# Experts on whole float32 weight slabs in column tiles, 36 slabs in a ring

## The chip, the cores and the metric

The kernel runs on one core of one Trainium2 chip. A core has TensorE (PE in the profile) for matrix products, VectorE (DVE), ScalarE (ACT), GpSimd (POOL), SyncE (SP), whose queue issues most transfers here, and 16 DMA engines. The metric is the device time of one execution in microseconds (us); lower is better.

## The reference

One layer of a decoder trunk on 512 tokens of 1024 channels, float32: a gated mixer, a cross attention, and a mixture of 32 experts of which each token takes 4. Only the last part is touched by the change:

```python
logits = xt @ w_router + b_router                  # (512, 32)
top_val, top_idx = lax.top_k(logits, 4)
gate = softmax(top_val)
def expert_block(xi, e):
    gu = xi @ w_gu[e] + b_gu[e]                    # 1024 -> 2048
    x_glu, x_lin = gu[..., ::2], gu[..., 1::2]
    x_glu = minimum(x_glu, 7.0)
    x_lin = clip(x_lin, -7.0, 7.0)
    h = x_glu * sigmoid(1.702 * x_glu) * (x_lin + 1.0)
    return h @ w_dn[e] + b_dn[e]                   # 1024 -> 1024
# y[token] += gate * expert_block(x[token], e); then h = layer_norm(2**0.25 * h + y)
```

An expert has 12.6 MB of weights (403 MB in all 32), in 24 slabs of 512 KB: 16 for gate and up, 8 for down. A slab is 128 input channels by 1024 outputs. With the reference's inputs its router gives the experts these numbers of tokens, in order: 49, 68, 94, 45, 50, 119, 41, 117, 131, 65, 9, 83, 52, 80, 73, 31, 73, 22, 27, 67, 85, 38, 45, 42, 144, 15, 147, 49, 58, 72, 21, 36. So 17 experts have up to 64, ten have 65 to 96, two have 97 to 128 and three have more.

## The kernel before, in words

`dense` (line 807) computes everything up to the router; `experts` (line 1205) then goes through the 32 experts in order, whatever their counts; `finish` (line 1468) does the last layer norm.

*Tokens in, rows out.* `route_expert` turns one-hot rows (made on GpSimd by `one_hots`, line 983) into the indices and gates of an expert's tokens. An indirect DMA on the GpSimd queue gathers them (line 1030), TensorE transposes them (`tokens`, line 1118), and at the end another indirect DMA adds the expert's rows into the `based` tensor in memory (line 1037). For up to 64 tokens both move half rows, so that 128 partitions are used.

*Two ways for the products* (`products`, line 1132). The counts are loaded into registers, and each engine branches on them. Up to 64 tokens: the float32 slab as it came is streamed against 64 columns of tokens, the two halves of the output in the two column halves of TensorE (line 1155). More than 64: each slab is first split into a float32r high part (ScalarE) and a float32r low part (VectorE) by `split` (line 126), and three float32r products take the place of the float32 one (`mm3`, lines 156 to 160). Above 128 tokens, the rest goes through four more float32r products a slab with tokens and their low parts packed side by side (lines 1163 to 1169).

*Order of the work.* Inside a hand-ordered section, per turn e: gate/up half 0 of expert e, routing of e + 2, the activation of half 0, gate/up half 1, transposes of the tokens of e + 1, the activation of half 1, the down product of e - 1, transposes of the hidden units of e, and the rows of e - 1 out. Between them stand calls of `ahead`, which issue the splits of coming slabs.

*Slabs.* Loads of 512 KB are issued in order on the SP queue (line 186) into a ring of 17 raw buffers; the split slabs have 8 pairs of buffers. The bias rows are loaded first of all (line 1210), in float32r.

Of the kernel before, what the change touches and what calls it, by code (L numbers as in the profile page):

```python
# [109 lines left out]
class Trunk:  # L110
# [42 lines left out]
    def ps(self, name, tag="c", dt=F32, shape=(512,)):  # L153
        return self.psum.tile([128] + list(shape), dt, name=name, tag=tag, bufs={"tp": 2, "f": 2, "c": 4, "ga": 2, "gb": 2, "y": 2}[tag])
# [652 lines left out]
    def dense(self):  # L807
        nc, tc, a = self.nc, self.tc, self.a
        with ExitStack() as es:
# [9 lines left out]
            self.xs = self.xg[:, 0:512]  # L819
# [34 lines left out]
            def finish():  # L854
                while done:
                    b, t = done.pop(0)
                    self.router_block(b, t)
                    if b == 3:
                        self.first = self.route_expert(0, self.route, self.one_hots(0, self.route))
                        self.router_end()  # L860
                    self.base_block(b, t)
# [10 lines left out]
            finish()  # L872


    def router_init(self):
# [23 lines left out]
        pid2 = p.tile([128, 1], F32, name="pid2")  # L899
        nc.gpsimd.iota(pid2, pattern=[[0, 1]], base=0, channel_multiplier=2, allow_small_or_imprecise_dtypes=True)  # L900

        self.offs = p.tile([128, 1], F32, name="offs")
        nc.gpsimd.memset(self.offs[0:64], 2.0 * NONE)
        nc.gpsimd.memset(self.offs[64:128], 2.0 * NONE + 1)
        for b in range(4):
            nc.gpsimd.tensor_copy(self.VT[:, b, :, 0], pid.to_broadcast([128, 32]))
            nc.gpsimd.memset(self.VT[:, b, :, 1], 128.0 * b - NONE)
            nc.gpsimd.tensor_copy(self.VT[:, b, :, 5], pid2.to_broadcast([128, 32]))
            nc.gpsimd.memset(self.VT[:, b, :, 6], 2 * (128.0 * b - NONE))

        self.esel = p.tile([128, 2, 32], F32R, name="esel")
# [4 lines left out]
        for j in range(2):  # L916
            nc.vector.tensor_scalar(self.esel[:, j], e, 0.0, None, op0=OP.is_equal)
        for r, j in ((slice(0, 64), 1), (slice(64, 128), 0)):
            nc.vector.memset(self.esel[r, j].bitcast(F32), 0.0)
# [69 lines left out]
    def route_expert(self, e, pool, oh, bank="tp"):  # L989
# [3 lines left out]
        for n, c in ((128, 0), (CAP - 128, 16)):  # L993
            for b in range(4):
                nc.tensor.matmul(o[:n, c:c + 8], oh[:, b, 128 * (c > 0):128 * (c > 0) + n], self.VT[:, b, e, :],
                                 start=b == 0, stop=b == 3)
        for b in range(4):
            for r in (slice(0, 64), slice(64, 128)):
                nc.tensor.matmul(o[r, 8:16], oh[:, b, 0:64], self.VT[:, b, e, :], start=b == 0, stop=b == 3)  # L999
        return self.slot(o[:, 0:8], pool, "m"), self.slot(o[:CAP - 128, 16:24], pool, "x"), self.slot(o[:, 8:16], pool, "s")  # L1000

    def slot(self, o, pool, t):
# [3 lines left out]
        if t == "s":  # L1006
            nc.vector.tensor_scalar(ix, o[:, 5:6], o[:, 6:7], self.offs, op0=OP.add, op1=OP.add)
        else:
            nc.vector.tensor_scalar(ix, o[:, 0:1], o[:, 1:2], float(NONE), op0=OP.add, op1=OP.add)  # L1009
# [4 lines left out]
    def cond(self, c, *engines):  # L1014
        return self.nc.values_load(c[0:1, 0:1], engines=engines, min_val=0, max_val=512,
                                   skip_runtime_bounds_check_because="a count of the 512 tokens")

    def gather_expert(self, count, route):

        with self.tc.If(self.cond(count, mybir.EngineType.Pool) < 65) as s:  # L1020
            self.gather(self.xs, route[2][0], True)
        with s.Else():
            self.gather(self.xg, route[0][0])

    def rows_of(self, t, halves):
        return (t.rearrange("t (h c) -> (t h) c", h=2), 1023) if halves else (t, 511)

    def gather(self, xg, ix, halves=False):
        src, last = self.rows_of(self.x2d, halves)
        return self.nc.gpsimd.indirect_dma_start(  # L1030
            out=xg, out_offset=None, in_=src, in_offset=bass.IndirectOffsetOnAxis(ap=ix[:, 0:1], axis=0),
            bounds_check=last, oob_is_err=False).ins

    def scatter(self, y, ix, halves=False):

        dst, last = self.rows_of(self.based, halves)
        self.nc.gpsimd.indirect_dma_start(  # L1037
            out=dst, out_offset=bass.IndirectOffsetOnAxis(ap=ix[:, 0:1], axis=0), in_=y, in_offset=None,
            bounds_check=last, oob_is_err=False, compute_op=OP.add)
# [27 lines left out]
    def x_tiles(self, xg, x=None, part=(0, 1)):  # L1067

        nc = self.nc
        x = x or self.mx.tile([128, 8, 2, 128], F32R, name="xe", tag="xe", bufs=self.XB)  # L1070
        for g in part:
            self.turn4(x[:, 4 * g:4 * g + 4], xg[:, ts(g, 512)], "xt")
        return x

    def turn4(self, out, src, name):

        pt = self.ps(name, "tp")
        for j in range(4):
            self.nc.tensor.transpose(pt[:, ts(j, 128)], src[:, ts(j, 128)], self.ident)
        self.split(out[:, :, 0], out[:, :, 1], pt.rearrange("p (k t) -> p k t", t=128))  # L1080

    def swiglu(self, pg, pl, g, l):
        nc = self.nc
        nc.vector.tensor_scalar(g, pg, 7.0, None, op0=OP.min)  # L1084
        a = nc.scalar.activation(g, g, AF.Gelu_apprx_sigmoid)  # L1085
        nc.vector.tensor_scalar(l, pl, 7.0, -7.0, op0=OP.min, op1=OP.max)
        v = nc.vector.scalar_tensor_tensor(l, l, 1.0, g, op0=OP.add, op1=OP.mult)
        return a.ins, v.ins

    def hidden_units(self, rv, p, more):  # L1090

        tc = self.tc
        g, l = [self.mx.tile([128, 512], F32, name=n, tag=n, bufs=self.SB[n]) for n in ("mg", "ml")]
        with tc.If(rv < 65) as s:
            self.swiglu(p[0][0:64], p[0][64:128], g[:64], l[:64])
        with s.Else():
            self.swiglu(*p, g, l)
            with tc.If(rv > 128):
                self.more_swiglu(*more, g)
        return l  # L1100

    def hidden(self, rv, units):

        nc = self.nc
        out = [self.mx.tile([128, 4, 2, 128], F32R, name="hx", tag="hx", bufs=self.HB) for _ in units]
        whole = [self.mx.tile([128, 4, 64], F32, name="hs", tag="hs", bufs=self.HB) for _ in units]
        with self.tc.If(rv < 65) as s:
            for t, u in zip(whole, units):
                pt = self.ps("hts", "tp")
                for j in range(4):  # L1110
                    nc.tensor.transpose(pt[:, ts(j, 64)], u[:64, ts(j, 128)], self.ident[:64, :64])
                nc.scalar.copy(t.rearrange("p k t -> p (k t)"), pt[:, :256])
        with s.Else():
            for t, u in zip(out, units):
                self.turn4(t, u, "ht")
        return out, whole

    def tokens(self, rv):

        nc = self.nc  # L1120
        out = self.mx.tile([128, 8, 2, 128], F32R, name="xe", tag="xe", bufs=self.XB)
        whole = self.mx.tile([128, 8, 64], F32, name="xw", tag="xw", bufs=self.XB)
        with self.tc.If(rv < 65) as s:
            pt = self.ps("xts", "tp")
            for j in range(4):
                nc.tensor.transpose(pt[:, ts(j, 128)], self.xs[:, ts(j, 128)], self.ident)  # L1126
            nc.scalar.copy(whole.rearrange("p (h g) t -> p h g t", h=2), pt.rearrange("p (g h t) -> p h g t", g=4, h=2))
        with s.Else():
            self.x_tiles(self.xg, out)
        return out, whole  # L1130

    def products(self, rv, p, lhs, small, more, pm, ws, bias=None, pack=None):

        nc, tc = self.nc, self.tc
        mm = nc.tensor.matmul
        if bias:
            sel, row, w = self.esel, bias[0], bias[1]

        def first():
            for k in range(8):
                for n in range(2):
                    if k == 0 and bias:
                        mm(p[n], sel[:, n, row:row + 1].to_broadcast([128, 128]), w, start=True, stop=False)
                    self.mm3(p[n], (lhs(k)[:, 0], lhs(k)[:, 1]), [w[:, ts(n, 512)] for w in ws(k)[:2]],
                             k == 0 and not bias, k == 7)

        with tc.If(rv < 65) as s:  # L1149
            for n in range(2 if bias else 0):  # L1150
# [376 lines left out]
```

## Time and profile before

| | us |
|---|---|
| median of 3 runs | 1934.29 |
| lowest and highest | 1933.17, 1937.43 |
| the profiled execution | 1926.95 |
| its span, first to last instruction | 1925.2 |

The rows further down come from that profiled execution. Times are from the start of its span. In a row of a timeline stand start, duration, engine, line, operation, what it writes and reads, how many were merged, and in brackets the idle time before it and what ended that. In a table by line stand total and mean duration after the bar. A float32 matmul shows as two records, a float32r or bf16 one as one. Busy time of TensorE includes time at the lower clock.

### The profile page before, as it was taken

To read this page: it belongs to the slowest core of one execution; us is meant where nothing else is said; L and a number is where in the kernel's file an instruction comes from. 1 tells how busy PE (TensorE), PEld (TensorE's weight loads), DVE (VectorE), ACT (ScalarE), POOL (GpSimd) and SP (SyncE) were. 2 spreads that over 40 slices of the span, in tenths; PEclk is the share of its full clock that TensorE was granted. 3 is DMA by queue.
4 is the path that set the end of the run, shared out by engine and by line. 5 is a ranking of instruction groups with operands and counts; after the bars stand their busy time and mean duration, and the time that the engine had idled before them with its cause. 6 is when DMAs were issued, how large, how long until landed. Compare 5 with 4: busy or idle time off the path is not lost. (4 is left out here: it accounts for less than half of the span.)

```text
span 1925.2 us, 27343 instructions
## 1 busy us (share of the span) xinstructions
PE 1701.1 (88%) x8236; PEld 1164.7 (60%) x8236; DVE 1056.0 (55%) x1747; ACT 813.0 (42%) x1252; POOL 352.6 (18%) x414
## 2 busy tenths in 40 slices
PE   8998999999996688889998888998898899897982
PEld 7666878778984365456675646664564365653540
DVE  7855776567564375337683746663573245442433
ACT  5567555344431254226463535452462134332321
POOL 1010003410011221112121212212122111111002
PEclk9999999999996799899999989999898999898986
DMA  4213235655232888989777899999899959589994
GB/s 165 99 57 113 97 107 169 194 184 184 89 113 80 333 343 322 371 307 397 278 277 279 301 370 337 360 375 397 346 375 355 401 211 369 188 333 351 351 346 174
DMA packets 148184, 505.16 MB, mean 262 GB/s; under 512 B 19856, under 2 KB 22448, under 8 KB 147888
## 3 DMA queue, kind: packets, MB, share of 16 engines
q1 hardware_dynamic: 131952, 460.38, 62.8%
q0 software_dynamic: 15936, 40.96, 7.3%
q8 instruction: 170, 2.79, 0.6%
q14 instruction: 126, 1.03, 0.1%
HBM read 481.86 MB, written 28.84 MB: 265 GB/s over the span
## 5 line engine op out<-in xcount | busy, mean ns | idle before, releaser
L128 DVE TENSOR_TENSOR wlo<-raw,whi 128x1024 fp32r<-128x1024 f32 (+2 forms) x441 | 510.6, 1199 | 209.5 <-ACT whi L128 137.2
L128 ACT CAST whi<-raw 128x1024 fp32r<-128x1024 f32 (+2 forms) x441 | 432.2, 1025 | 238.6 <-PE gu L160 41.9
L1155 PE MATMUL gu<-raw,xw 128*64 128x512 f32 x1088 | 249.5, 611 | 0.0
L158 PE MATMUL gu<-whi,xe 128*128 128x512 f32 x480 | 194.7, 406 | 8.2 <-ACT whi L128 8.2
L159 PE MATMUL gu<-wlo,xe 128*128 128x512 f32 x480 | 194.0, 404 | 5.6 <-DVE mg L1084 4.3
L160 PE MATMUL gu<-whi,xe 128*128 128x512 f32 x480 | 193.6, 403 | 2.5 <-issue 2.5
L1155 PEld LDWEIGHTS gu<-raw,xw 128*64 128x64 f32 x1088 | 89.9, 142 | 157.9 <-issue 143.8
L986 POOL TENSOR_SCALAR oh<-places,pm 128x192 bf16<-128x192 bf16 x128 | 141.4, 1113 | 225.9 <-PE sl L999 203.2
L1085 ACT ACTIVATE mg<-mg 128x512 f32<-128x512 f32 (+1 forms) x70 | 44.2, 631 | 267.0 <-DVE mg L1084 259.2
L158 PE MATMUL y<-whi,hx 128*128 128x512 f32 x240 | 101.7, 424 | 29.7 <-ACT whi L128 17.0
L1155 PE MATMUL y<-raw,hs 128*64 128x512 f32 x544 | 122.2, 602 | 1.1 <-issue 1.1
L158 PEld LDWEIGHTS gu<-whi,xe 128*128 128x128 f32 x480 | 94.3, 196 | 31.6 <-ACT whi L128 8.6
L160 PEld LDWEIGHTS gu<-whi,xe 128*128 128x128 f32 x480 | 93.7, 195 | 27.2 <-issue 5.5
L159 PEld LDWEIGHTS gu<-wlo,xe 128*128 128x128 f32 x480 | 93.9, 196 | 23.0 <-DVE wlo L128 1.0
L160 PE MATMUL y<-whi,hx 128*128 128x512 f32 x240 | 100.1, 417 | 3.8 <-issue 3.8
L159 PE MATMUL y<-wlo,hx 128*128 128x512 f32 x240 | 100.0, 417 | 2.2 <-DVE wlo L128 2.2
L1009 DVE TENSOR_SCALAR ixm<-sl 128x1 int32<-128x1 f32 x32 | 7.0, 220 | 165.9 <-PE sl L999 161.3
L1084 DVE TENSOR_SCALAR mg<-gu 64x512 f32<-64x512 f32 (+1 forms) x64 | 43.4, 677 | 97.8 <-PE xts L1126 47.2
L1155 PEld LDWEIGHTS y<-raw,hs 128*64 128x64 f32 x544 | 38.9, 138 | 72.8 <-issue 62.8
L1037 POOL DMA_INDIRECT based<-ysb,ixm x15 | 24.2, 1611 | 283.1 <-ACTq L1345 137.1
L158 PEld LDWEIGHTS y<-whi,hx 128*128 128x128 f32 x240 | 48.7, 203 | 42.8 <-ACT whi L128 21.5
L1037 POOL DMA_INDIRECT based<-ysb,ixs x17 | 27.4, 1614 | 178.6 <-ACTq L1149 89.0
(500 smaller groups left out, 3191.9 us busy)
## 6 DMA issues: line engine op xcount, KB each, us to landing
raw<-in_wgu SPq DMA_DIRECT2D x512, 512.0 KB
raw<-in_wdn SPq DMA_DIRECT2D x256, 512.0 KB
raw<-in_wt SPq DMA_DIRECT2D x27, 512.0 KB
tgd<-tg POOLq DMA_DIRECT2D x16, 256.0 KB, 2.6
raw<-in_wck SPq DMA_DIRECT2D x8, 512.0 KB
tgr<-tgd POOLq DMA_DIRECT2D x16, 256.0 KB, 3.1
raw<-in_wmix SPq DMA_DIRECT2D x8, 512.0 KB
raw<-in_wcv SPq DMA_DIRECT2D x8, 512.0 KB
```

What stands on the lines that cost most here:

```text
L128: return nc.scalar.copy(hi, src).ins, (lo_eng or nc.vector).tensor_sub(lo, src, hi.bitcast(F32)).ins
L158: mm(out, w[0], x[0], start=start, stop=False)
L159: mm(out, w[0], x[1], start=False, stop=False)
L160: mm(out, w[1], x[0], start=False, stop=stop)
L986: self.nc.gpsimd.tensor_scalar(oh[:, b], self.places, self.pm[:, b, e:e + 1], None, op0=OP.is_equal)
L1009: nc.vector.tensor_scalar(ix, o[:, 0:1], o[:, 1:2], float(NONE), op0=OP.add, op1=OP.add)
L1037: self.nc.gpsimd.indirect_dma_start(out=dst, out_offset=bass.IndirectOffsetOnAxis(ap=ix[:, 0:1], axis=0), in_=y, in_offset=None, bounds_ch ...
L1084: nc.vector.tensor_scalar(g, pg, 7.0, None, op0=OP.min)
L1085: a = nc.scalar.activation(g, g, AF.Gelu_apprx_sigmoid)
L1155: mm(p[0][64 * n:64 * n + 64], small(k), ws(k)[2][:, ts(n, 512)], start=k == 0 and not bias, stop=k == 7)
```

## The change

- The splits into high and low parts go, with their buffers; every expert uses the float32 slabs as loaded.
- One gate/up phase an expert instead of two: gate and up of all 1024 hidden units are summed in four PSUM banks at once, the slabs in the order k by k. The down product of e - 1, the transposes and the rows out follow as before.
- Three shapes by count. Up to 64: two 64-column tiles side by side, as before. 65 to 96: tiles of 32 columns, three for a half of the outputs, twelve a k, laid over the four column strips; in the down product two k share one bank's strips. 97 and more: 128 columns. Above 128, the rest goes through the 64-column shape as well.
- The buffers of the split parts join the raw ones: a ring of 36 slabs, 3 + 6 of them in buffers that the dense layers use, 27 in room that they leave. First fetch: 36 slabs, ahead of the bias rows; then 16 after each gate/up and 8 after each down product.
- The bias is added by bf16 matmuls of three parts at the end of each sum, not at its start. The parts are made by `bias_rows`; in the second half it includes the + 1 of the reference.
- The gate weights are multiplied into the hidden units (`units`); the rows out are copied by VectorE and ScalarE, and gathers and scatters always move whole rows.

```diff
+    def slab(self, src):
+        p, tag, dt = self.turn("s")
+        raw = p.tile([128, 1024], dt, name="raw" if dt == F32 else tag, tag=tag)
+        raw = raw if dt == F32 else raw.bitcast(F32)
+        self.nc.sync.dma_start(raw, src)
+        return raw
...
+    def up_small(self, e, b, x, w):
+        part = [slice(0, 64), slice(64, 128)]
+        for k in range(8):
+            for j in range(2):
+                for h in range(2):
+                    mm(b[j][part[h]], x[:, k], w(h, k)[:, ts(j, 512)], start=k == 0, stop=False)
+        for j in range(2):
+            for h in range(2):
+                self.bias(e, 64, h, j, b[j][part[h]])
+
+    def up_96(self, e, b, x, w):
+        tiles = [(h, 0, g, b[h][32 * g:32 * g + 32]) if g < 3 else (h, 1, 2, b[h][96:128]) for h in range(2) for g in range(4)]
+        tiles += [(h, 1, g, b[2][64 * h + 32 * g:64 * h + 32 * g + 32]) for h in range(2) for g in range(2)]
+        for k in range(8):
+            for h, j, g, o in tiles:
+                mm(o, x[:, k, 32 * g:32 * g + 32], w(h, k)[:, ts(j, 512)], start=k == 0, stop=False)
+        for h, j, g, o in tiles:
+            self.bias(e, 32, h, j, o)
+
+    def up_128(self, e, b, x, w):
+        for k in range(8):
+            for j in range(2):
+                for h in range(2):
+                    mm(b[2 * j + h], x[:, k], w(h, k)[:, ts(j, 512)], start=k == 0, stop=False)
...
+    def down_96(self, b, h, w):
+        tiles = [(0, g, b[0][32 * g:32 * g + 32]) for g in range(3)] + [(1, 2, b[0][96:128])]
+        for k in range(0, 8, 2):
+            for i in range(2):
+                for n, g, o in tiles:
+                    mm(o, h[:, k + i, 32 * g:32 * g + 32], w(k + i)[:, ts(n, 512)], start=k + i == 0, stop=k + i == 7)
+            for i in range(2):
+                for g in range(2):
+                    r = 64 * i + 32 * g
+                    mm(b[1][r:r + 32], h[:, k + i, 32 * g:32 * g + 32], w(k + i)[:, 512:1024], start=k == 0, stop=k == 6)
...
+    def bias_rows(self):
+        for h in range(2):
+            raw = p.tile([128, 2, 512], F32, name="bguraw", tag=("mg", "ml")[h], bufs=1)
+            for i in range(4):
+                nc.sync.dma_start(raw[32 * i:32 * i + 32], self.a["bgu"][:, ts(h, 1024)].rearrange("e (j c) -> e j c", j=2))
+            nc.vector.tensor_scalar(raw[:, 1], raw[:, 1], 1.0, None, op0=OP.add)
+            t = p.tile([128, 2, 512], BF, name="bgu", tag="bgu", bufs=2)
+            nc.scalar.copy(t, raw)
+            for first in (32, 64):
+                for r in (slice(a, a + 32) for a in range(first, 96, 32)):
+                    nc.vector.tensor_sub(raw[r], raw[r], t[r])
+                    nc.scalar.copy(t[r], raw[r])
...
+        fetch(len(self.ring["s"][0]))
+        more_gather(0)
+        x = self.tokens(rv[0][0])
+        self.bias_rows()
...
             for e in range(33):
                 f = e - 1
                 if e < 30:
                     routing(e + 2)
+                    rv[e + 2] = conds(count[e + 2])
                 if e < 32:
+                    b, bm = self.up(rv[e][0], e, x, lambda h, k: slabs[e, h, k])
+                    fetch(16)
                 if e < 31:
+                    x = self.tokens(rv[e + 1][0])
                 if e < 30:
+                    self.gather(self.xg, route[e + 2][0][0])
+                    more_gather(e + 2)
                 if e < 32:
+                    l = self.units(rv[e][1], b, bm, route[e])
+                if 0 < e:
+                    by, bym = self.down(rv[f][0], h[f], mh[f], lambda k: slabs[f, 2, k])
+                    fetch(8)
                 if e < 32:
+                    h[e] = self.hidden(rv[e][0], l)
+                    mh[e] = m["h"]
+                if 0 < e:
+                    self.rows_out(rv[f][1], rv[f][2], by, bym, route[f])
...
+                self.ring["s"] = [[(wraw, "raw", F32)] * 3 + [(whl, t, F32R) for t in ("whi", "wlo") for _ in range(3)] +
+                                  [(wraw2, "raw", F32)] * self.NRAW, 0]
```

`up` and `down` branch on the count: first, above 128, the 64-column shape on the rest; then one of the three shapes.

## Rows read from the trace of the kernel before

**Rows 1.** The page, slices: TensorE's clock in tenths, busy share of the DMA engines

```profile
PEclk9999999999996799899999989999898999898986
DMA  4213235655232888989777899999899959589994
```

**Rows 2.** Stretches: us, busy PE, PEld, DVE, ACT, POOL; clock, DMA share, GB/s

```profile
620.00:1890.00 1270.00, 1112.33 (x5288) 694.14 (x5288) 636.63 (x845) 498.26 (x622) 249.00 (x226) 0.93 0.88 332
...
940.00:1000.00 60.00, 60.00 (x283) 45.34 (x283) 43.52 (x54) 36.69 (x44) 9.98 (x8) 1.00 0.65 235
1500.00:1540.00 40.00, 34.12 (x176) 12.98 (x172) 10.43 (x20) 8.02 (x13) 8.35 (x9) 0.96 1.03 400
1890.00:1925.00 35.00, 0.00 (x0) 0.00 (x0) 17.64 (x28) 6.65 (x9) 11.40 (x13) 0.54 0.42 150
```

**Rows 3.** Waits of the SP queue, 620 to 1900 us: total, times, longest

```profile
SPq L186 <- PE gu L158: 220.0, 24, 20.3
SPq L186 <- DMA raw<-in_wgu: 175.8, 177, 3.2
SPq L186 <- PE gu L1169: 116.2, 6, 30.0
```

**Rows 4.** Timeline of the SP queue, 1480 to 1560 us

```profile
1491.35 21.25 SPq L186 DMA_DIRECT2D raw<-in_wgu  x16
...
1546.92 0.33 SPq L186 DMA_DIRECT2D raw<-in_wdn  x1
```

**Rows 5.** Timelines of TensorE and of its weight loads, several stretches

```profile
680.13 0.41 PE L995 MATMUL sl<-VT,oh 128*128 128x8 bf16 x6
...
681.93 0.40 PE L158 MATMUL gu<-whi,xe 128*128 128x512 f32 x1
...
692.04 0.39 PE L160 MATMUL gu<-whi,xe 128*128 128x512 f32 x1
...
700.26 1.09 PE L1079 MATMUL ht<-ident,ml 128*128 128x128 f32 x8
...
868.01 7.07 PE L1155 MATMUL gu<-raw,xw 128*64 128x512 f32 x32
...
890.85 0.71 PE L1111 MATMUL hts<-ident,ml 64*128 64x64 f32 x8
...
1500.21 0.14 PEld L1155 LDWEIGHTS y<-raw,hs 128*64 128x64 f32 x2 [0.29 <-issue]
```

**Rows 6.** Line 1155's records: duration in ns, shortest, median, longest

```profile
L1155 PE MATMUL gu<-raw,xw x1088: 589/592/1061, 637.8 to 1873.7; 128*64 128x512 f32 x182
```

**Rows 7.** Indirect gathers by kind: how many, us to landing

```profile
xg<-x2d,ixs POOLq DMA_INDIRECT x17, 6.8
...
xg<-x2d,ixm POOLq DMA_INDIRECT x15, 8.5
...
mrxg<-x2d,ixx POOLq DMA_INDIRECT x3, 6.6
```

**Rows 8.** TensorE's waits, 620 to 1890 us; of eleven on "issue" the first and last

```profile
PE y L158 <- ACT whi L128: 17.0, 5, 7.4
...
PE sl L995 <- issue: 9.6, 4, 2.9
...
PE gu L159 <- issue: 0.8, 1, 0.8
```

**Rows 9.** Table by line and shape, 640 to 1900 us: busy us, mean ns

```profile
L128 DVE TENSOR_TENSOR wlo<-raw,whi 128x1024 fp32r<-128x1024 f32 x360 | 423.8, 1227 | 165.9 <-ACT whi L128 93.8 <-PE gu L159 39.0 <-PE y L160 10.8
L128 ACT CAST whi<-raw 128x1024 fp32r<-128x1024 f32 x360 | 357.0, 1047 | 161.4 <-PE gu L160 41.9 <-DMA raw<-in_wdn 38.3 <-issue 22.9
...
L1086 DVE TENSOR_SCALAR ml<-gu 128x512 f32<-128x512 f32 x30 | 20.3, 676 | 0.0
```

**Rows 10.** Timeline of the SP queue, 540 to 650 us

```profile
619.68 2.62 SPq L1210 DMA_DIRECT2D bguraw<-in_bgu  x4
622.47 24.07 SPq L186 DMA_DIRECT2D raw<-in_wgu  x22
```

More of the change, by code (lines that the diff above doesn't have):

```diff
@@ L1012, in slot, with gather, scatter @@
         return ix, g
[L1014 to L1029, printed above, removed]
+    def gather(self, xg, ix):
         return self.nc.gpsimd.indirect_dma_start(
[L1031 to L1036, printed above, removed]
+            out=xg, out_offset=None, in_=self.x2d, in_offset=bass.IndirectOffsetOnAxis(ap=ix[:, 0:1], axis=0),
+            bounds_check=511, oob_is_err=False).ins
+    def scatter(self, y, ix):
         self.nc.gpsimd.indirect_dma_start(
-            out=dst, out_offset=bass.IndirectOffsetOnAxis(ap=ix[:, 0:1], axis=0), in_=y, in_offset=None,
-            bounds_check=last, oob_is_err=False, compute_op=OP.add)
+            out=self.based, out_offset=bass.IndirectOffsetOnAxis(ap=ix[:, 0:1], axis=0), in_=y, in_offset=None,
+            bounds_check=511, oob_is_err=False, compute_op=OP.add)
     def base_block(self, b, x2):
@@ L1082, in swiglu, with turned @@
[L1082 to L1090, printed above, removed]
+    def turned(self, src, n, name):
+        rows = src.shape[0]
+        pt = self.ps(name, "tp")[:, :n * rows]
+        for j in range(n):
+            self.nc.tensor.transpose(pt[:, ts(j, rows)], src[:, ts(j, 128)], self.ident[:rows, :rows])
+        return pt
@@ new lines, in bias @@
+    def bias(self, e, n, half, j, out):
+        self.nc.tensor.matmul(out, self.esel[:, e:e + 1].to_broadcast([128, n]), self.bgu[half][:, j], start=False, stop=True)
+    def up_small(self, e, b, x, w):
+        mm = self.nc.tensor.matmul
+        part = [slice(0, 64), slice(64, 128)]
[6 more added lines that the diff above has]
+                self.bias(e, 64, h, j, b[j][part[h]])
@@ new lines, in up_128, with up @@
+    def up_128(self, e, b, x, w):
+        mm = self.nc.tensor.matmul
+        for k in range(8):
[3 more added lines that the diff above has]
+        for h in range(2):
+            for j in range(2):
+                self.bias(e, 128, h, j, b[2 * j + h])
+    def up(self, rv, e, x, w):
+        tc, m = self.tc, self.more
+        b = [self.ps("gu", "gu") for _ in range(4)]
+        bm = [self.ps("gux", "y") for _ in range(2)]
+        with tc.If(rv > 128):
+            self.up_small(e, bm, m["x"], w)
+        with tc.If(rv < 65) as s:
+            self.up_small(e, b, x[:, :, 0:64], w)
+        with s.Else():
+            with tc.If(rv < 97) as t:
+                self.up_96(e, b, x, w)
+            with t.Else():
+                self.up_128(e, b, x, w)
+        return b, bm
@@ L1092, in hidden_units, with down_128, down @@
+    def down_128(self, b, h, w):
+        for k in range(8):
+            for n in range(2):
+                self.nc.tensor.matmul(b[n], h[:, k], w(k)[:, ts(n, 512)], start=k == 0, stop=k == 7)
+    def down(self, rv, h, mh, w):
         tc = self.tc
-        g, l = [self.mx.tile([128, 512], F32, name=n, tag=n, bufs=self.SB[n]) for n in ("mg", "ml")]
+        b = [self.ps("y", "y") for _ in range(2)]
+        bm = self.ps("yx", "gu")
+        with tc.If(rv > 128):
+            self.down_small(bm, mh, w)
@@ L1094, in hidden_units @@
         with tc.If(rv < 65) as s:
-            self.swiglu(p[0][0:64], p[0][64:128], g[:64], l[:64])
+            self.down_small(b[0], h[:, :, 0:64], w)
         with s.Else():
[L1097 to L1112, printed above, removed]
-        with s.Else():
-            for t, u in zip(out, units):
-                self.turn4(t, u, "ht")
-        return out, whole
@@ L1118, in tokens @@
[L1118 to L1130, printed above, removed]
@@ L1174, in pack @@
-    def pack(self, out, src, n, half=0):
-        nc = self.nc
-        pt = self.ps("mt", "tp")
-        r = slice(64 * half, 64 * half + 64)
-        for j in range(n):
-            nc.tensor.transpose(pt[:, ts(j, 64)], src[:, ts(j, 128)], self.ident[r, r])
-        v = pt[:, :n * 64].rearrange("p (k t) -> p k t", t=64)
-        self.split(out[:, :, 0:64], out[:, :, 64:128], v)
-    def fold(self, t, p):
-        self.nc.scalar.copy(t, p[64:128])
-        self.nc.vector.tensor_add(t, t, p[0:64])
@@ L1205, in experts, with cond @@
+    def cond(self, c, *engines):
+        return self.nc.values_load(c[0:1, 0:1], engines=engines, min_val=0, max_val=512,
+                                   skip_runtime_bounds_check_because="a count of the 512 tokens")
     def experts(self):
         nc, tc, a = self.nc, self.tc, self.a
-        p = self.mx
-        raw = self.turn("r").tile([128, 2, 512], F32, name="bguraw", tag="raw")
-        for i in range(4):
-            nc.sync.dma_start(raw[32 * i:32 * i + 32], a["bgu"].rearrange("e (h j c) -> e h j c", h=2, j=2)[:, :, i // 2])
@@ L1250, in number, with fetch @@
+        slabs, self.nfetch = {}, 0
+        def fetch(n):
+            for e, part, k in order[self.nfetch:self.nfetch + n]:
+                slabs[e, part, k] = self.slab(a["wdn"][e, k] if part == 2 else a["wgu"][e, part, k])
+            self.nfetch += n
         def number(e):
@@ L1298, in routing @@
                 self.oh = self.one_hots(e + 1, self.mx)
+        count = {0: number(0), 1: number(1)}
+        route, rv, h, mh = {0: self.first}, {0: conds(count[0])}, {}, {}
+        fetch(len(self.ring["s"][0]))
+        more_gather(0)
+        x = self.tokens(rv[0][0])
+        self.bias_rows()
         self.oh = self.one_hots(1, self.mx)
-        with tc.manual_schedule(engines={getattr(mybir.EngineType, n) for n in self.MANUAL}):
+        with tc.manual_schedule(engines={PE, DVE, ACT, POOL}):
@@ L1480 @@
     FP = 0, 2
+    NRAW = 27
     W0, KF, MID = 2, 0, 6
```

342 lines of the change are left out of this document (145 added, 197 removed).

## The prediction

> **What bounds the kernel now.** I read the page's slices first: in the right two thirds the rows of TensorE's clock and of the DMA engines both go up and down, seldom in the same slice [rows 1]. An average over that says little, so next came busy time by stretch [rows 2]. Up to 620 us the dense layers run, which the change hardly touches. From 620 to 1890 us the 32 experts run: TensorE is busy 1112 of 1270 us at a mean granted clock of 0.93, the DMA engines move 332 GB/s. Two stretches inside show the two limits: from 940 to 1000 us TensorE has no gap and the clock is 1.00 while the DMAs move 235 GB/s; from 1500 to 1540 us the DMAs are full at 400 GB/s and TensorE has gaps. So the stage alternates between both bounds, because 17 raw slabs in hand are less than one expert (24). The waits of the load queue say the same: the longest are for TensorE and for landed transfers in turn [rows 3].
>
> What each bound alone would need, at its best: the stage moves 332 GB/s x 1270 us = 422 MB, which at 400 GB/s is 1054 us. The load queue's own pace agrees: 40 slabs from 1491.35 to 1546.92 us, 1.39 us each, so 768 slabs take 1067 us [rows 4]. TensorE at the full clock is added up below. The clock has two levels, 2.4 and 1.2 GHz; a mean of 0.93 is 14% of 1270 us at the lower one, 178 us, which cost up to 89 us. It falls where TensorE waits (0.54 from 1890 us on, when no matmul runs; 0.96 from 1500 to 1540 us, beside gaps).
>
> **The change, part by part.** 65 to 128 tokens: three float32r products per slab half go, one float32 product comes. Before, one float32r matmul follows the other every 0.23 us (the first and the last of 45 in a row start at 681.93 and 692.04 us), so three are 0.69 us and an expert 48 x 0.69 = 33 us [rows 5]. The float32 price stands in the small experts: 32 records, 16 matmuls of 64 tokens in pairs side by side, take 7.07 us, 0.884 us a pair [rows 5]. A 128-wide float32 matmul has the same 512 columns and the same two records; I take 0.884 us. Bounds: two records of at least 0.589 us, 1.18 us, if nothing of them overlapped [rows 6]; no row has 1024 columns of float32 in less than the pair's 0.884. That is 48 x 0.884 = 42.4 us for 97 to 128 tokens: dearer than before, by 9 us.
>
> For 65 to 96 tokens the new code lays twelve tiles of 32 tokens over four column strips: 24 sets of four per gate/up phase, 12 in the down product. No row shows four strips at once. If four run as two do, a set costs 0.884 us and an expert 36 x 0.884 = 31.8 us; if only two run at a time, 63.6 us. The nearest row is the pair: its two weight loads are over in 0.14 us together, a third of the 0.44 us that a record has [rows 5], so I take full overlap and keep the other end for the range.
>
> The sum for TensorE, with the counts of the section on the reference (17 up to 64, ten of 65 to 96, two of 97 to 128, three above, which agree with 17, 15 and 3 indirect transfers [rows 7]): 17 x 21.2 + 10 x 31.8 + 5 x 42.4 + 3 x 21.2 (the tokens beyond 128) = 360 + 318 + 212 + 64 = 954 us. Before it was 360 + 15 x 33 + 3 x 22 (48 x 2 x 0.23) = 921 us. So the change takes no arithmetic off TensorE; it adds 33 us. Around it each expert has routing matmuls (16, some 0.5 us), transposes of tokens and of hidden units (0.71 us for a small, 1.09 for a large expert, each) [rows 5] and the bias (now bf16; 2 to 4 slots of 0.23 us): 17 x 2.4 + 15 x 3.5 + 3 x 2.2 (transposes and bias of the rest) = 100 us. TensorE's waits for its own instructions, 37.3 us in eleven rows of the table of waits [rows 8], I keep, as there are as many branches. Together 1091 us.
>
> The splits go: 360 casts on ScalarE and 360 subtractions on VectorE, 357 and 424 us [rows 9]. TensorE's idle 158 us hold waits for them (the longest, of the down product, 17.0 us [rows 8]), and a slab could not be reissued before its split. VectorE and ScalarE keep the gate: at 0.68 us an operation [rows 9] the chain is 2.7 us for a small expert and some 5 us for a large one. It runs beside the previous expert's down product (7.07 us or more), which now stands right behind gate/up; if that cover were short, TensorE would stand for the rest at every expert.
>
> The ring goes from 17 raw slabs to 36, an expert and a half. With it, a small expert's surplus of loading time (33 us of loads, 21 of matmuls) is paid from slabs fetched under a large one. I stepped the counts through a ring of 36 with 1.39 us a slab: past the third expert TensorE never waits for a slab. What is late next is TensorE itself: 1091 us against 1054 to 1067.
>
> The Trainium skill, page "DMA: Bandwidth & Descriptors", section Specifications, gives an HBM limit of about 358 GB/s a core; 422 MB at that would be 1178 us, and the loads, not TensorE, would set an end near 1830 us. The 40 us at 400 GB/s here speak against it [rows 2].
>
> The start gets worse. The bias rows' loads stood ahead of the slabs on the SP queue (619.68 us); now they are behind the first 36, of which I count nine as early (their buffers, on the left side, fall free with the dense layers), 27 x 1.39 = 38 us from 622.5 us [rows 10]. Then come two casts and six subtractions and copies in line, about 12 us by the 1.05 and 1.23 us of such operations [rows 9]. Expert 0's gate/up ends in its bias matmuls, and everything on TensorE is queued behind them: it stands from about 645 to 676 us. The slabs go on landing meanwhile, so this costs TensorE's chain only. `router_end` moves behind the last base block: four small matmuls and three copies, so the counts come some 5 us later, under the same wait for slabs. On POOL's queue nothing new stands ahead of a gather: it still waits for the token transposes, a whole turn before its rows are needed, and the unconditional gathers and whole scatter rows add about 2 us each to a transfer (6.8 against 8.5 us to landing [rows 7]), beside matmuls. The rows out are one copy on each of two engines, as long as the one on ScalarE before.
>
> From 676 us: 1091 - 17 (expert 0's gate/up, done) = 1074, so the last matmul ends at 1750 us. The tail from 1890 to 1925 us is unchanged, 35 us [rows 2]: 1785 us. For the clock I add half of the idle time that is left (37 us of instruction waits), as before 89 went with 158: 20 us. Span 1805 us; the profiled execution has 1.75 us around its span and lies 7 us under the median shown, so I say 1812 us for a median.
>
> **The rivals.**
> 1. *Four strips run two at a time.* The place is the ten experts of 65 to 96 tokens, the price 31.8 us each, 318 us: about 2130 us, slower. It decides from 12 us an expert on, a set of 1.2 us instead of 0.884. For it: the pair moves two 4-byte streams, four strips would move four, and no row shows that. Against: the overlapped loads [rows 5].
> 2. *Four strips overlap in part.* A quarter of the way from 0.884 us to the 1.77 of two pairs a set costs 1.1 us, 36 x 0.22 x 10 = 80 us: about 1890 us. The Trainium skill, page "TensorE: Matmul & The Clock Gate", section Part 3 (measured speedup), has three column tiles at 2.38 instead of 3, a factor of 1.26; no run here shows it.
> 3. *The loads set the end.* If TensorE is better than my sum (no instruction waits, no standing at the bias), 622.5 - 12 (nine early slabs) + 1067 + 35 gives 1713 us at the least; with gaps in the loads as before, up to 1770 us.
> 4. *The new room is not used.* If reissue still lags TensorE's release as now, the 332 GB/s stay and so do 1270 us: about 1930 us, no change. The queue's waits of up to 30.0 us [rows 3] speak for it, the removed split stage against.
>
> **How the numbers follow.** Forecast 0.62 (own range 1770 to 1870), rival 1 0.14, rival 2 0.10, rival 3 0.08, rival 4 0.06. Out of the range stay rival 1 and the worst of 4: low 1740, high 1925. A measurement of this kernel tells about 0.2%, 4 us. Faster takes the forecast, rivals 2 and 3 and a little of 4: 0.81; same 0.03; slower 0.16.
>
> **What would show it.** TensorE's clock near 1.00 and busy over 95% from 700 us on; 32 records of 64-wide float32 still in 7.07 us; sets of four 32-wide records every 0.44 us (0.88 would be rival 1); a stand of some 30 us before expert 0's first bias matmul; the load queue waiting mostly for TensorE; DMAs near 390 GB/s. A mean DMA share of 1.0 with gaps on TensorE would be rival 3, a clock still at 0.93 would refute my sum.

## The result, and the profile after

The changed kernel takes 2028.04 us (2023.22 to 2032.33, 4 runs), the kernel before beside it 1935.59 us (4 runs). The ratio is 1.0478, 95% interval 1.0451 to 1.0505: slower, where 1812 us was forecast, and outside the range. The profiled execution has a span of 2021.5 us.

The busy time by stretch of the changed kernel (us, busy PE, PEld, DVE, ACT, POOL, clock, DMA share, GB/s) answers to [rows 2]:

```profile
620.00:1985.00 1365.00, 1115.65 (x6471) 433.47 (x6476) 169.84 (x377) 121.98 (x206) 188.12 (x225) 0.90 0.83 308
1985.00:2021.00 36.00, 0.19 (x2) 0.00 (x0) 18.35 (x29) 6.55 (x9) 11.41 (x13) 0.55 0.34 122
```

The tail is as long as before, and VectorE and ScalarE are relieved (637 to 170 us, 498 to 122 us). But the stage of the experts grew from 1270 to 1365 us. TensorE's busy time hardly moved (1112 to 1116 us); its idle time went from 158 to 249 us, and the clock fell from 0.93 to 0.90. The DMA engines carry 308 GB/s and have room. So neither bound of the prediction holds: TensorE stands, and for slabs only in a small part (some 43 of the 249 us by its table of waits). The page's slices (TensorE's clock, busy share of the DMA engines) show the lower clock over the whole right part, as against [rows 1]:

```profile
PEclk9999999999986598897999999999998989999896
DMA  5213335653437579987756889999989979498793
```

What TensorE waited for in the changed kernel between 620 and 1985 us (total, times, longest) answers to [rows 8]:

```profile
PE gu L1075 <- ACT bgu L1269: 31.3, 2, 25.0
PE xt L1056 <- issue: 30.9, 11, 5.5
...
PE gu L1096 <- issue: 15.6, 6, 6.5
PE xts L1056 <- issue: 14.2, 6, 2.4
PE gu L1105 <- issue: 11.4, 4, 7.7
```

The first line is the stand at the bias rows, which was forecast at 31 us. The others are new in size. "Issue" means that the engine waited for nothing that the profile shows. Over the stage all rows on "issue" sum to some 94 us in 36 stops, before to 37.3 us in 16. The timeline of TensorE in the changed kernel shows where they stand (start, duration, what, and in brackets the idle time before it):

```profile
678.00 1.01 PE L1075 MATMUL gu<-bgu,esel 128*64 128x512 bf16 x3 [6.37 <-ACT bgu L1269]
684.46 1.94 PE L1056 MATMUL xt<-ident,xg 128*128 128x128 f32 x8 [5.45 <-issue]
...
694.92 22.54 PE L1096 MATMUL gu<-raw,xe 128*32 128x512 f32 x192 [0.64 <-PEq L1115]
717.28 0.82 PE L1075 MATMUL gu<-bgu,esel 128*32 128x512 bf16 x12
718.03 1.09 PE L1056 MATMUL xt<-ident,xg 128*128 128x128 f32 x8
...
735.68 4.61 PE L1096 MATMUL gu<-whi,xe 128*32 128x512 f32 x24 [6.29 <-issue]
```

Each stop on "issue" shown here follows a jump. At 684.46 us expert 0, with 49 tokens, has done its 64-wide branch and TensorE goes on behind the code of the 32-wide and the 128-wide shape, after 5.45 us. After the 32-wide branch of expert 1 the same step comes with no stop (718.03): there only the shorter 128-wide code lies between. The stop of 6.29 us stands where expert 2 enters its 32-wide branch, behind the 64-wide code and that for more than 128 tokens; expert 1 did the same at 694.92 us for 0.64 us. So not every jump stops for long, and what tells them apart these rows don't say; the section on why the prediction was wrong comes back to it.

The same timeline answers the question behind rivals 1 and 2: 192 records, 24 sets of four strips, in 22.54 us are 0.94 us a set; four 32-column strips of float32 run side by side.

The waits of the load queue in the changed kernel, against [rows 3]:

```profile
SPq L184 <- DMA raw<-in_wgu: 201.4, 197, 3.3
SPq L184 <- PE gu L1105: 180.9, 80, 22.3
SPq L184 <- PE gu L1096: 177.9, 42, 35.2
```

It waits for TensorE as before, up to 35.2 us at a time. In the 32-wide shape the slabs come free only late in the phase, and that was the rival explanation at this point (theory R below).

### The profile page after: what moved, and what is told of

It reads as the page before. It is cut to its first block, busy times and chain, and to the rows that moved or that the text cites. A ratio compares the mean times of both kernels' runs of the same rounds, so it can differ in the third digit from the quotient of the medians.

```text
span 2021.5 us, 26184 instructions
## 1 busy us (share of the span) xinstructions
PE 1705.6 (84%) x9419; PEld 904.9 (45%) x9424; DVE 589.9 (29%) x1277; ACT 437.0 (22%) x836; POOL 294.3 (15%) x405
## 5 line engine op out<-in xcount | busy, mean ns | idle before, releaser
L1084 PE MATMUL gu<-raw,xe 128*64 128x512 f32 x864 | 209.3, 619 | 13.1 <-PEq L1115 10.0
L1096 PE MATMUL gu<-raw,xe 128*32 128x512 f32 x1560 | 178.2, 598 | 5.3 <-PEq L1115 2.4
L1084 PEld LDWEIGHTS gu<-raw,xe 128*64 128x64 f32 x864 | 70.7, 142 | 135.6 <-issue 128.2
L1011 POOL DMA_INDIRECT xg<-x2d,ixm x32 | 35.6, 1112 | 633.3 <-PEq L1217 341.0
L1105 PE MATMUL gu<-raw,xe 128*128 128x512 f32 x240 | 106.4, 601 | 8.1 <-issue 8.1
L1096 PEld LDWEIGHTS gu<-raw,xe 128*32 128x32 f32 x1560 | 53.2, 111 | 120.9 <-issue 115.1
L1202 PE MATMUL y<-raw,hs 128*32 128x512 f32 x592 | 92.3, 674 | 13.4 <-DMA wlo<-in_wdn 7.1
L128 DVE TENSOR_TENSOR wlo<-raw,whi 128x1024 fp32r<-128x1024 f32 (+2 forms) x81 | 86.9, 1075 | 47.9 <-ACT whi L128 47.6
L128 ACT CAST whi<-raw 128x1024 fp32r<-128x1024 f32 (+2 forms) x81 | 75.3, 931 | 84.1 <-issue 18.9
L1068 ACT COPY xe<-xt 128x512 f32<-128x512 f32 x30 | 16.4, 588 | 335.2 <-PE xt L1056 335.2
L1211 PE MATMUL y<-raw,hs 128*128 128x512 f32 x144 | 67.2, 627 | 4.3 <-ACT mg L1128 4.3
L160 PE MATMUL g<-xTh,wlo 128*128 128x512 f32 x128 | 52.4, 410 | 2.8 <-DVE wlo L128 2.8
L1075 PE MATMUL gu<-bgu,esel 128*32 128x512 bf16 (+2 forms) x203 | 27.0, 384 | 31.6 <-ACT bgu L1269 31.3
## 6 DMA issues: line engine op xcount, KB each, us to landing
raw<-in_wdn SPq DMA_DIRECT2D x230, 512.0 KB, 10.5
```

Of the source, the lines that this page charges most:

```text
L128: return nc.scalar.copy(hi, src).ins, (lo_eng or nc.vector).tensor_sub(lo, src, hi.bitcast(F32)).ins
L160: mm(out, w[1], x[0], start=False, stop=stop)
L1011: return self.nc.gpsimd.indirect_dma_start(out=xg, out_offset=None, in_=self.x2d, in_offset=bass.IndirectOffsetOnAxis(ap=ix[:, 0:1], axis= ...
L1084: mm(b[j][part[h]], x[:, k], w(h, k)[:, ts(j, 512)], start=k == 0, stop=False)
L1096: mm(o, x[:, k, 32 * g:32 * g + 32], w(h, k)[:, ts(j, 512)], start=k == 0, stop=False)
L1105: mm(b[2 * j + h], x[:, k], w(h, k)[:, ts(j, 512)], start=k == 0, stop=False)
```

## The experiments

Three theories stood. **R**: slabs are given back late in the 32-wide shape, so the ring does not help. **L**: the loads bind. **J**: TensorE stops at jumps until the code behind them has come, and the change lays more code behind each jump (a third shape, unrolled in gate/up and down). The ratios are to the kernel before, timed beside each.

**No branches at all.** The counts of this input stand in the program, so each expert's code holds its own shape alone.

```diff
-        with tc.If(rv < 65) as s:
+        if rv < 65:      # likewise every branch in tokens, up, units, hidden, down, rows_out
```

> The changed kernel with each expert's shape fixed in the program by this input's counts, instead of branches at run time: no engine jumps in the expert stage, and no code of shapes that are not taken. Arithmetic, slabs, ring and order are the same. Theory J (TensorE stops at its branches until the code behind the jump has come, 2.3 to 7 us each): TensorE's idle time from 620 us on falls from 250 us to under 100, time 1810 to 1870 us. Theory R (the shape for 65 to 96 tokens gives its slabs back too late, because the branches share one count) also wants it faster, since without branches each slab counts for itself. Theory L (the loads bind): no more than 30 us faster, 2000 us.

Measured: 1786.56 us, ratio 0.9238 (0.922 to 0.9256), 241 us less than the changed kernel with the same loads and the same products, and less than the 1810 us at which J's range began. Its stretch:

```profile
620.00:1750.00 1130.00, 1059.62 (x6474) 401.28 (x6476) 169.90 (x377) 118.71 (x206) 188.33 (x225) 0.97 0.98 369
```

Idle 70 us instead of 249, the clock 0.97 instead of 0.90, 369 GB/s instead of 308. Of the 235 us that the stretch is shorter, 179 are idle time and 56 busy time; the matmuls being the same, the 56 us go with the clock. So the loads did not bind the changed kernel, and L falls. J and R both wanted this run faster, so it does not tell them apart.

**Late give-back.** The branch-free form with the strips of the 32-wide shape in two passes, so that all 16 slabs come free in the last third.

```diff
-        for k in range(8):
-            for h, j, g, o in tiles:
+        for some in (tiles[:8], tiles[8:]):
+            for k in range(8):
+                for h, j, g, o in some:
```

> The one before, but in the 65-to-96 shape the last four of the twelve tiles run for all eight k behind the first eight tiles, so that each gate/up slab is given back only in the last third of the phase, as late as in the changed kernel. Theory R: most of what the fixed shapes won is lost again, 1930 us or more. Theory J: within 20 us of the kernel with fixed shapes.

Measured: 1790.68 us, 4 us more. With 36 slabs in the ring and no branches, giving slabs back late costs next to nothing, though the load queue's longest wait for this shape goes from 13.5 to 23.8 us. So R falls as the cause of the 241 us, as far as the branch-free form can tell.

**The bias rows first.** The changed kernel with the bias rows asked for ahead of the slabs.

```diff
+        self.bias_rows()
         fetch(len(self.ring["s"][0]))
...
-        self.bias_rows()
```

> The changed kernel with the bias rows loaded and cut into parts ahead of the first 36 slabs. All theories that have TensorE as the bound (J, R): the stand of 31 us before expert 0's bias goes, 20 to 30 us faster, 2000 us. Theory L: the same time within 5 us, as TensorE makes the stand good later.

Measured: 1988.24 us, ratio 1.03 (1.0261 to 1.0339), 40 us less than the changed kernel. That is more than the 20 to 30 us expected: the stand of 31.3 us was on the path, and the clock of the stage is 0.92 instead of 0.90. It does not turn the sign.

**Without the 32-wide shape.** More than 64 tokens all take 128 columns; the third shape leaves the program.

```diff
-            with tc.If(rv < 97) as t:
-                self.up_96(e, b, x, w)
-            with t.Else():
-                self.up_128(e, b, x, w)
+            self.up_128(e, b, x, w)      # likewise in units, hidden, down, rows_out
```

> The changed kernel without the shape for 65 to 96 tokens: those ten experts run in the 128-column shape. It adds 10 x 10.6 = 106 us of matmuls, takes about half of the gate/up code away and lets every slab go k by k. Theory R: its stalls (150 us or more) go, 1980 us or less. Theory J: the jumps stay and only the code skipped in each is shorter, 2060 to 2130 us. If four strips overlapped only in part: no slower than 2028 us.

Measured: 1952.5 us, ratio 1.0097 (1.0076 to 1.0119). By the shapes this is more matmul work (12 sets of some 0.87 us more for each of ten experts, 104 us), yet it takes 76 us less than the changed kernel: the shape costs more by being in the program than it saves. By itself this number is what R wanted (1980 us or less) and misses J's 2060 to 2130 us, because J had the price of skipped code too low; the next run tells the two apart.

**The 32-wide shape present, and never taken.** Every expert runs exactly what it runs in the experiment above.

```diff
-            with tc.If(rv < 97) as t:
+            with tc.If(rv < 1) as t:     # all five places
```

> The changed kernel with the code of the 65-to-96 shape still in the program, but under a condition that no count meets (below 1): all experts above 64 run in the 128-column shape, as in the run without that shape, and every engine jumps over the unused code. The work done is that of the run without the shape (1952.5 us). Theory J (jumps over code): the unused code costs nearly what the shape cost in the changed kernel, 2030 to 2080 us. Theory R (late give-back, which needs the shape to be run): 1940 to 1965 us.

Measured: 2188.93 us, ratio 1.1344 (1.1299 to 1.1389), 236 us more than without that code, far above J's 2030 to 2080 us and out of reach of R's 1940 to 1965. This is the plainest run of the study: same arithmetic, same loads, 7.4 us more an expert for code that only has to be jumped over. The two stretches, first without the code, then with it:

```profile
620.00:1915.00 1295.00, 1164.26 (x4476) 510.32 (x4476) 149.66 (x353) 118.89 (x197) 189.88 (x226) 0.96 0.89 324
```

```profile
620.00:2150.00 1530.00, 1222.89 (x4476) 524.85 (x4476) 149.11 (x348) 118.76 (x196) 187.88 (x222) 0.89 0.78 274
```

Both have 4476 matmul records. Idle time grows from 131 to 307 us, busy time by 59 us at a clock of 0.89 instead of 0.96. TensorE's longest waits, with the code present (620 to 2150 us):

```profile
PE gu L1105 <- issue: 91.8, 16, 9.4
PE xt L1056 <- issue: 32.7, 11, 5.5
...
PE y L1211 <- issue: 27.2, 4, 10.5
```

and without it (620 to 1915 us), where the first of these shrinks to a sixth:

```profile
PE gu L1105 <- issue: 15.5, 4, 6.3
```

Line 1105 is the 128-wide gate/up, line 1211 the 128-wide down product. With the unused code in front of them, TensorE stands up to 9.4 and 10.5 us.

**The kernel before, without branches.** The same edit as in the first experiment, on the kernel before.

```diff
-            with tc.If(cond(c, POOL) > 128):
+            if c > 128:                  # likewise every branch on a count
```

> The kernel before the change with each expert's branch fixed in the program by this input's counts; splits, slabs and order as they were. Theory J: the kernel before paid for its jumps too, but less (37 us of instruction waits in its table and some of its other idle time), so 1860 to 1895 us, and the change alone, without branches on either side, is worth 75 to 105 us. If branches were no cost in the kernel before: 1925 to 1935 us.

Measured: 1817.1 us, ratio 0.9404 (0.9373 to 0.9436), lower than the 1860 to 1895 us expected. Its stretch:

```profile
620.00:1775.00 1155.00, 1082.99 (x5268) 658.67 (x5268) 635.39 (x845) 496.49 (x622) 252.66 (x225) 0.97 0.95 362
```

So the kernel before also paid for its branches at run time and what hangs on them, some 118 us, and the changed one 241. Without branches the change is worth 1817 - 1787 = 30 us, not the 75 to 105 us expected. TensorE's idle time is 72 us here, against 158 us with branches, although every split is still in place.

**A lean version.** Without the 32-wide shape, with the bias rows first, and the code for more than 128 tokens nested inside the branch for more than 64, so that small experts pass it in one jump.

These lines show the nesting alone:

```diff
-        with tc.If(rv > 128):
-            self.up_small(e, bm, m["x"], w)
         with tc.If(rv < 65) as s:
             self.up_small(e, b, x[:, :, 0:64], w)
         with s.Else():
+            with tc.If(rv > 128):
+                self.up_small(e, bm, m["x"], w)
```

> The changed kernel with less to jump over: no 65-to-96 shape, the code for the rest beyond 128 tokens inside the branch for more than 64 (a small expert skips both in one jump), and the bias rows ahead of the slabs. Theory J: 1952 us less 30 to 40 for the bias and 10 to 30 for the jumps, 1885 to 1915 us, below both kernels. Theory L: no lower than 1940 us.

Measured: 1925.82 us, ratio 0.9964 (0.9945 to 0.9983), some 10 us above what J expected, below L's 1940, and 9 us (0.4%) under the kernel before.

**Only the nesting.** The changed kernel with that last edit alone: one jump fewer for a small expert, the same code behind it.

```diff
-        with tc.If(rv > 128):            # up, units, down, rows_out
         with tc.If(rv < 65) as s:
...
         with s.Else():
+            with tc.If(rv > 128):
```

> The changed kernel with one edit: the code for the rest beyond 128 tokens stands inside the branch for more than 64 tokens, so that the 17 small experts skip it in the same jump as the other shapes, in four places a turn. Theory J by number of jumps: 17 experts x 2 jumps of TensorE x some 2 us less, 1950 to 1990 us. Theory J by the amount of code skipped (which stays the same): 2015 to 2035 us.

Measured: 2022.48 us, 6 us less than the changed kernel. It is not the number of jumps that makes most of the loss.

**Shorter jumps.** The changed kernel, with the branches of gate/up and down cut into four.

```diff
+        for ks in [range(k, k + 2) for k in range(0, 8, 2)]:
             with tc.If(rv > 128):
-                self.up_small(e, bm, m["x"], w)
+                self.up_small(e, bm, m["x"], w, ks)    # likewise the other shapes, and down
```

> The changed kernel with the same shapes and the same code, but the branches around the gate/up and the down matmuls are cut into four, one for every two k slabs: four times as many jumps, each over a quarter of the code. If TensorE stops at a jump in proportion to the code in that jump beyond what it already holds, short jumps are nearly free and the time falls to 1880 to 1960. If what counts is the sum of skipped code, however cut, it stays at 2010 to 2050. If each jump has a price of its own, it rises above 2080.

Measured: 2003.85 us, ratio 1.037 (1.0343 to 1.0397): 24 us less, between the first two cases and much nearer to the second. The timeline of TensorE, split kernel, says why it lies between:

```profile
698.88 5.36 PE L1096 MATMUL gu<-raw,xe 128*32 128x512 f32 x48 [0.64 <-PEq L1116]
704.87 5.36 PE L1096 MATMUL gu<-raw,xe 128*32 128x512 f32 x48 [0.64 <-PEq L1116]
710.86 5.36 PE L1096 MATMUL gu<-raw,xe 128*32 128x512 f32 x48 [0.64 <-PEq L1116]
716.03 0.84 PE L1075 MATMUL gu<-bgu,esel 128*32 128x512 bf16 x12
716.80 1.09 PE L1056 MATMUL xt<-ident,xg 128*128 128x128 f32 x8
718.74 1.94 PE L1193 MATMUL y<-raw,hs 128*64 128x512 f32 x8 [0.85 <-PEq L1219]
721.00 1.94 PE L1193 MATMUL y<-raw,hs 128*64 128x512 f32 x8 [0.32 <-PEq L1219]
```

In the place of one long stop there are now several of 0.3 to 0.9 us, one at each seam (the end of a quarter, where TensorE branches again). Adding up the gaps of the timelines over the stage of the experts, without the first stand at the bias rows (25.0 and 23.3 us):

| gaps of TensorE | 2 to 12 us | below 2 us |
|---|---|---|
| changed kernel | 39, 149.6 us | 98, 76.4 us |
| split in four | 7, 28.1 us | 284, 178.6 us |

Some 121 us of long stops go, 102 us of short ones come, 186 of them at some 0.55 us. The clock does gain, as the stretches show (0.96 instead of 0.90):

```profile
620.00:1960.00 1340.00, 1110.50 (x6453) 397.22 (x6460) 169.96 (x378) 122.02 (x206) 189.67 (x226) 0.96 0.87 313
```

So a branch has two prices here: about half a microsecond for itself, and several microseconds more at some of those that skip much.

**The lean version, split.** The same cut on the lean version, whose quarters are short.

```diff
+        for ks in [range(k, k + 2) for k in range(0, 8, 2)]:
             with tc.If(rv < 65) as s:
...
             with s.Else():
                 with tc.If(rv > 128):
...
                 self.up_128(e, b, x, w, ks)
```

> The version without the 32-wide shape (bias rows ahead of the slabs, code beyond 128 tokens nested; 1925.82 us) with its gate/up and down branches cut into four as well. By the price per length of a jump 1840 to 1900, below both kernels; by the sum of skipped code 1915 to 1940; by the price per jump above 1950.

Measured: 1897.76 us, ratio 0.9823 (0.9798 to 0.9848), at the upper end of the expected band. With the counts read at run time it beats both kernels: 1.8% under the kernel before, 6% under the changed one. Its stretch has 68 us of idle time and the clock near full:

```profile
620.00:1855.00 1235.00, 1167.35 (x4451) 484.76 (x4468) 148.51 (x347) 117.41 (x196) 190.42 (x222) 0.99 0.92 338
```

**Branch-free, with the bias rows first.** The first and the third edit together:

```diff
-        with tc.If(rv < 65) as s:
+        if rv < 65:
...
+        self.bias_rows()
         fetch(len(self.ring["s"][0]))
```

> The branch-free form of the changed kernel (1786.56 us) with the bias rows asked for ahead of the 36 slabs. If TensorE's work sets its time, the bias stand of some 31 to 40 us comes off: 1745 to 1757. If there, without the stops, the slab loads set the end (369 GB/s over the stretch), little is gained: 1772 to 1790.

Measured: 1765.05 us, ratio 0.9133 (0.9109 to 0.9156): 21.5 us off, between the two theories. Its stretch:

```profile
620.00:1725.00 1105.00, 1064.16 (x6457) 399.87 (x6464) 170.26 (x377) 118.63 (x206) 189.43 (x222) 0.99 0.99 377
```

Here both bounds are met at once: TensorE is busy for 1064 of 1105 us, and the DMA engines are full (0.99). The stand was 34.1 us in the branch-free kernel; that the loads kept the rest of it from being gained is argued from the 0.99, not shown.

## Why the prediction was wrong

**The step that failed** is in the sum for TensorE: "TensorE's waits for its own instructions, 37.3 us in eleven rows of the table of waits, I keep, as there are as many branches." I counted branches. What sets the stops is how much code lies behind them, and the change put a third shape there, unrolled, of which the 32-wide one alone has 192 matmul records in gate/up. The runs put the price of the branches at 118 us in the kernel before and 241 us in the changed one, where the sum had 37.3 us of waits and 20 us of clock: some 184 of the 216 us between forecast and measurement. (The 123 us by which the two prices differ, less the 30 us that the change is worth without branches, are the 93 us between the medians; that holds by arithmetic.) The 37.3 us were too small already for the kernel before: the rows on "issue" hold only part of these stops, since others of the same size are put down to a transfer or another semaphore, and the lost clock stands in no row of waits.

**The gain was put down to the wrong thing too.** The prediction says "TensorE's idle 158 us hold waits for them", the splits. With the branches fixed and the splits left in, 72 us of idle time are left of the 158. So more than half of the idle time that the change was to win back hung on the branches, which it kept.

**What a stop waits for.** The Trainium skill, page "Runtime: NRT & Kernel Launch", section "Instruction fetch mechanics", has the rule that I did not weigh: an engine's instructions are streamed ahead in order, in blocks of 16 KiB or 256 instructions, and a taken branch to a target outside what is held must wait for its block. The trace agrees. The profile's row for the queue q8 (packets, MB, share), in the expert stage of the branch-free changed kernel:

```profile
q8 instruction: 51, 0.84, 0.3%
```

51 packets of 16.4 KB for 12950 records of TensorE (matmuls and weight loads) are one for 254, so q8 carries TensorE's code. The same row in the changed kernel and, to the digit, in the kernel with the unused shape, then without the shape:

```profile
q8 instruction: 168, 2.75, 0.8%
```

```profile
q8 instruction: 94, 1.54, 0.5%
```

The shape has 384 records in gate/up and 192 in the down product of each expert, some 73 packets in all by 254 a packet; 74 more are fetched, whether it is run or jumped over. So skipped code is loaded all the same. And the stops are in step with these packets. For each stop of TensorE of 2 to 12 us in the stage, the trace gives the time from the last q8 packet that landed in it to the next matmul:

| | stops of 2 to 12 us | go on 1.3 to 2.1 us after a packet |
|---|---|---|
| kernel before | 28 | 19 |
| changed kernel | 39 | 32 |
| unused shape | 47 | 42 |
| without the shape | 8 | 4 |
| split in four | 7 | 1 |
| branch-free, changed | 6 | 0 |
| branch-free, before | 8 | 0 |

With the packets' times shifted at random against the stops, some 4 of the changed kernel's 39 would match, at most 12 in 500 tries. In the kernel with the unused shape the 29 stops that hold one packet last 2.6 us in the median, the 13 that hold two 7.8 us. The two cases of the timeline above fit: in the 6.29 us before 735.68 a packet is under way from 733.0 to 734.1 us, in the three microseconds before 694.92 none. So most long stops are waits for code, and they last longer where two packets have to come. Why one jump finds its code at hand and the next does not stays open. The short stops at the branches are another thing: in the split kernel, with 178 packets in the stage, they make up 179 of its 230 us of idle time.

**The clock.** I added 20 us for it, on the assumption of 37 us of stops. With 249 us of idle time the clock was 0.90. That term hung on the failed one: without branches it is 0.97, with the bias first as well 0.99.

**What held.** Matmuls of 954 + 100 us: the branch-free kernel with the bias first is busy for 1064 us at 0.99, within 1%. The 0.884 us that I took for a set of four strips: 0.94 us in the changed kernel's first such expert, and 128 records in 13.94 us, 0.87 us a set, in the branch-free kernel at full clock. The 128-wide matmul at 0.884 us: 32 records in 13.90 us, 0.87 us each. The timeline of TensorE in the branch-free kernel:

```profile
955.11 13.90 PE L1212 MATMUL y<-raw,hs 128*128 128x512 f32 x32
...
971.22 13.94 PE L1097 MATMUL gu<-raw,xe 128*32 128x512 f32 x128
```

So rivals 1 and 2 are out. The Trainium skill, page "TensorE: Matmul & The Clock Gate", section Part 3, gives a factor of 2.38 for three column tiles; the trace does not show such a loss: here four strips cost what two did. The stand at the bias was forecast from 645 to 676 us and runs, in two pieces, from 646 to 678; the bias rows first are worth 40 us. The ring: with the stops gone the loads reach 369 GB/s and the late give-back costs 4 us, so rival 4 is out as a mechanism. The tail is 36 us.

**Forecast against runs, branch-free.** 1812 us forecast, 1787 measured; that they lie so near is in part luck. Without the 37.3 us of stops and the 20 us of clock, which a kernel without branches does not have, my sum is 1755 us, 32 us too low. That is mostly idle time that the sum had at nothing: beside the stand at the bias the branch-free kernel stands for some 36 us, 20 of them for slabs, where my stepping of the ring had none past the third expert. Rival 3 (1713 to 1770 us) is what one gets once the stops and the bias stand both go: 1765 us, the DMA engines at 0.99. The Trainium skill, page "DMA: Bandwidth & Descriptors", section Specifications, gives a limit of about 358 GB/s a core; the trace does not agree for this program on one core: 377 GB/s over 1105 us.

**The test in the prediction** worked: "a clock still at 0.93 would refute my sum". It is 0.90, and TensorE is busy for 82% of the stage where over 95% was wanted.

## What to carry to other kernels

Where each engine branches at run time, count the instructions that a jump skips, not the branches alone: a further unrolled shape costs every item that does not take it, 7.4 us an expert here. Build the kernel once with the choices fixed: its time tells what the change itself is worth (30 us here) and what the branches take (118 and 241 us). If they take much, drop the shape whose code costs more than its matmuls save (here the longest one, though ten experts used it), and then cut what is left into short branches. Together with the bias rows first and the nesting that gave 1898 us, the best of the versions with run-time counts. The kernel before was not given short branches, so how much of its own 118 us they would give back is open.

## What the runs showed of the hardware that was not expected

- Code that never runs is loaded and costs time: 74 packets more on the instruction queue and 236 us between two kernels with the same 4476 matmul records, in stops of up to 10.5 us on TensorE.
- A long stop at a jump ends 1.3 to 2.1 us after a packet of the instruction queue has landed (42 of 47 stops with the unused shape), though the table of waits names nothing, or a semaphore, as what ended it.
- With about the same idle time (249 and 230 us) the granted clock was 0.90 in the changed kernel, where long stops make up most of it, and 0.96 in its split form, where short ones do. This is one pair of runs.
- A set of four 32-column float32 strips takes as long as two 64-column ones or one matmul of 128 columns: 0.87, 0.88 and 0.87 us for 512 streamed columns.
